# Dense tiles with all products of first weight parts ahead of second ones, inputs normalized one per tile, second weight parts on VectorE in the output, final stores on two queues

## The chip, the cores and the metric

The kernel runs on one core of a Trainium2 chip. Its engines are TensorE (PE in the profile; its weight loads are listed apart as PEld), VectorE (DVE), ScalarE (ACT), GpSimd (POOL) and SyncE (SP), which here only starts DMA transfers. Each engine works through its own list of instructions in a fixed order, and waits at an instruction until what it needs has been made by the others. The metric is the time of one execution on the device in microseconds; three runs of the kernel before took 1370.2, 1366.8 and 1364.27 us, the median is 1366.8 us.

## The reference

One step of a decoder with one layer, for 64 sample tokens (8 sequences of 8) and a prompt of 512 tokens, 576 in all; the width is 1024. Two mixers work on one projection and are added to the residual: a state-space mixer (Mamba-2, 16 heads of 64) and a delta-rule mixer (RWKV-7, 16 heads of 64). A gated feed-forward part (2816 wide) and a per-layer embedding follow.

```python
hn = rmsnorm(h, norm_mix)
z, xbc, dt, rw = split(hn @ w_in)
y_ssd  = rmsnorm_per_group(ssd(conv(xbc), dt) * silu(z)) * ssd_norm
u      = rw + (previous_row(rw) - rw) * shift_mu      # token shift
r, k, v, w_lo, a_lo, g_lo = split(u)
gate   = sigmoid(g_lo) @ g2
y_rwkv = (head_norm(wkv(r, k, v, decay(w_lo), a(a_lo))) + bonus) * gate
h = h + [y_ssd ; y_rwkv] @ w_out
h = h + (silu(rmsnorm(h) @ w_gate) * (rmsnorm(h) @ w_up)) @ w_down
h = h + sigmoid(rmsnorm(h) @ w_ple_gate) * (p @ w_ple_proj)
y = rmsnorm(h, norm_final)                            # and the new states
```

## The kernel before

Channels lie on the 128 partitions and the 576 tokens along the free axis; a matmul takes one half of the tokens (288 columns). A dense product keeps nearly full float32 precision by a split: a weight `w` and an input `x` are each written as a first part (rounded for TensorE) and a second part (what the rounding left out), and three products are added up in PSUM: first times first, first times second, second times first. `mm3` (L211 to L215) issues these three for one k-tile of 128 input channels and one half, so L213 and L214 use the first weight part `whi` and L215 the second, `wlo`.

`linear` (L217 to L224) makes one output tile of 128 channels. It fetches the weights in chunks of four k-tiles (`wload`, which calls `wsplit`, L189 to L199): SyncE starts a DMA into `raw` (three buffers), ScalarE copies it to `whi` (L92), and GpSimd and VectorE in turn subtract to make `wlo` (L198). `whi` and `wlo` have two buffers each, so the parts of the next chunk can be made while the products of this one run. PSUM holds two dense tiles at a time.

The stages are, with their places in the profiled span:

- Start (0 to 60 us). The input arrives, its first parts without the norm (`xu`) feed the first tiles, and the norm's factor is put in behind them (L341). `norm_x(n)` (L330) normalizes `n` input tiles on VectorE (L332) and splits them for the later dense tiles. `gate_in` makes the gate's input, `gates` (L416 to L426) eight small dense tiles from it.
- Mixers (60 to 690 us). Four quarters of heads. `fill` (L451) takes the next dense tile off a list and is called in between the mixers' steps; `fill_for` makes sure that the six tiles of a quarter are there. `outp` (L787) reads out the state of the delta rule. `head_norm` (L865 to L897) normalizes; that of the last quarter splits its result into the list `YR` (L897, second parts on GpSimd).
- Residual tiles of the delta-rule mixer (670 to 790 us), whose inputs partly come back from memory (`yl<-yr_d`).
- State-space mixer's end and its output (790 to 870 us). `scaled` (L1292) makes one output tile from four k-tiles, that is one chunk, scales it by `STD` (the tiles `bc`, L1297) and adds it to the residual `h` (L1298); `after` (L1275) splits the new `h` and squares it for the next norm. The loops at L1301 to L1305 run the first half of the inputs for all eight channels and then the second half.
- Feed-forward (870 to 1150 us, L1319 to L1333) and down projection (1150 to 1295 us, L1335 to L1341), whose 22 k-tiles make chunks of 4, 4, 4, 4, 4 and 2.
- Embedding gate (L1352 to L1392) in two parts, columns 0 to 320 and 320 to 576, and the final norm. All 16 stores of `yT` (L1392) start on SyncE's queue.

What the source lists is not what the engines execute in that order. A scheduler with a simulated timeline lays down the order of each engine's instructions when the kernel is built, and the buffers decide what may overlap. So a change in one place can alter the order everywhere behind it. ScalarE needs another table of functions when it goes from one group of functions to another (`ACT_TABLE_LOAD`); the square root of the norms has its own.

Of the kernel before, what the change touches and what calls it, by code (L numbers as in the profile page):

```python
# [8 lines left out]
F32 = mybir.dt.float32  # L9
# [65 lines left out]
def hybrid_step(ctx, tc, A):  # L75
# [15 lines left out]
    def act(out, in_, func=AF.Copy, scale=1.0, bias=0.0):  # L91
        S.activation(out, in_, func, bias=bias, scale=scale)  # L92

# [80 lines left out]
    wat = [0]  # L174
    flip = [0]

    def split(src, pool, tags, shape, lo_eng=None, hi=None, lo=None, hi_eng=None, **kw):
# [11 lines left out]
    def wsplit(src, n, hi=None, lo=None):  # L189
# [6 lines left out]
        flip[0] += 1  # L196
        eng = G if flip[0] % 2 else V
        eng.tensor_tensor(lo[:, 0:n], raw[:, 0:n], hi[:, 0:n].bitcast(F32), ALU.subtract)  # L198
# [18 lines left out]
    def linear(xs, ps):  # L217
        nk = len(xs)
        for k in range(0, nk, 4):
            b = min(4, nk - k)  # L220
            hi, lo = wload(b)
            for i in range(b):
                xh, xl = xs[k + i]
                mm3(ps, hi[:, i * P:(i + 1) * P], lo[:, i * P:(i + 1) * P], xh, xl, k + i == 0, k + i == nk - 1)  # L224

# [201 lines left out]

    norm_x(3)
    ugh = gate_in()
    norm_x(5)  # L430

# [287 lines left out]
    def chain(s):  # L719
# [67 lines left out]
        def outp(g):  # L787
            sv = suv(g)
            ow = outs[g]
            for jj in jj2:  # L790
                for e in range(2):
                    T.matmul(ow[H[e], jj], sv[:, jj, 1, e], Gt[:, g, jj, 1, e], start=False, stop=True,  # L792
                             skip_group_check=True)
            act(AR[:, :, g], ow)

# [70 lines left out]
    def head_norm(s, ahead=()):  # L866
# [18 lines left out]
        for jj in jj2:  # L885
# [10 lines left out]
            else:  # L896
                YR.append(split(y, xp, ("xhi", "xlo"), [P, NT], lo_eng=G))  # L897

# [5 lines left out]
    for s in Q:  # L904
        if s.q == 0:
            fill(2)
            gates(ugh)
        fill_for(s)
# [390 lines left out]

    st = {"x": []}  # L1300
    for c in range(8):  # L1301
        scaled(c, 0)
    for c in range(8):
        scaled(c, 1)
        after(c, hs[c], "norm_ffn", me, "xs", 8, st)  # L1305
    if not RS1:
        rs = rstd_of(st)
# [44 lines left out]
    for a, b in ((0, 320), (320, NT)):  # L1352
        n = b - a
        acc = None
        for c in range(8):
# [15 lines left out]
            V.tensor_tensor(t, ps, rs[:, a:b], ALU.mult)  # L1371
            act(t, t, AF.Sigmoid)
            V.tensor_tensor(t, t, PL[c][:, a:b], ALU.mult)  # L1373
# [11 lines left out]
        for c in range(8):  # L1385
# [4 lines left out]
            else:  # L1390
                V.scalar_tensor_tensor(h, h, par("norm_final", c), ps, ALU.mult, ALU.mult)
            nc.sync.dma_start(A["yT"][c, :, a:b], h)  # L1392

# [131 lines left out]
```

## Time and profile before

| what | value |
|---|---|
| median of three runs | 1366.8 us |
| the profiled execution | 1370.43 us, span 1368.7 us |
| TensorE busy, mean granted clock | 1259.1 us (92%), 0.947 |
| VectorE, ScalarE, GpSimd busy | 719.6, 577.4, 550.2 us |
| dense products (L213 to L215, all inputs) | the three costliest groups: 450.8, 447.9 and 447.7 us |
| `wlo` subtract (L198) | GpSimd 136 x 1344 ns, VectorE 136 x 724 ns |

The profiled execution is one of the slower ones of this kernel. Busy time of matmuls overlaps: a matmul is listed with 0.29 us though the next one starts sooner, so the spacing of the starts tells the rate. The clock is the one granted to TensorE, as a share of its higher level.

### The profile page before, as it was taken

What the parts mean: (1) busy time and instruction counts of PE and PEld (TensorE: products, weight loads), DVE (VectorE), ACT (ScalarE), POOL (GpSimd) and SP (SyncE); (2) the same over time, 40 slices, a digit from 0 to 9 for tenths busy, and PEclk for the clock granted to TensorE, in tenths of its full rate; (3) what the DMA queues carried; (4) which work ended last, traced back from release to release, by engine and by line L of the source; (5) the groups of instructions that cost most, each with busy time, mean ns of one, the idle gap of its engine ahead of it and who ended that gap; (6) DMA issues with size and microseconds to landing.
All of it is one profiled execution on the core that took longest, in us unless ns stands there. A gap on an engine that the chain in (4) does not pass through costs nothing.

```text
span 1368.7 us, 26325 instructions
## 1 busy us (share of the span) xinstructions
PE 1259.1 (92%) x10565; PEld 1160.4 (85%) x10565; DVE 719.6 (53%) x1333; ACT 577.4 (42%) x1148; POOL 550.2 (40%) x543
## 2 busy tenths in 40 slices
PE   6897999999989979899989979999999999999986
PEld 5786897789868857777779769999999999999985
DVE  7648766787687785843367676522222221111255
ACT  6565345634653553344425364432332332222253
POOL 5326414632454153133456676432332332334332
PEclk9997899899979989989999989999999999999998
DMA  4322342234223312362644532233232222222432
GB/s 162 124 70 62 85 119 60 81 100 128 61 90 91 101 58 84 88 209 82 189 145 142 183 97 71 70 85 79 84 85 81 83 85 77 82 80 79 148 92 69
DMA packets 94458, 135.56 MB, mean 99 GB/s; under 512 B 34704, under 2 KB 39056, under 8 KB 94336
## 3 DMA queue, kind: packets, MB, share of 16 engines
q1 hardware_dynamic: 94336, 133.88, 32.8%
q8 instruction: 83, 1.36, 0.4%
q14 instruction: 39, 0.32, 0.1%
HBM read 106.10 MB, written 27.75 MB: 98 GB/s over the span
## 4 chain that ended last, share of the span: by engine, by line
PE 60%; DVE 15%; ACT 5%; DMA 5%; issue 4%; POOL 3%; DVEq 0%; SPq 0%; ACTq 0%; POOLq 0%
PE lin L215 16%; PE lin L213 16%; PE lin L214 16%; DVE h L375 2%; DVE Tt L656 1%; DVE tmp L654 1%; DMA raw<-wts 1%; POOL wlo L198 1%; DVE suv L809 1%; PE cx L777 1%; PE lin L593 1%; PE cx L769 1%; DVE wlo L198 1%; PE cx L792 1%; DVE pg L1373 1%
## 5 line engine op out<-in xcount | busy, mean ns | idle before, releaser
L213 PE MATMUL lin<-xhi,whi 128*128 128x288 f32 (+1 forms) x1488 | 450.8, 303 | 3.3 <-ACT whi L92 2.2
L215 PE MATMUL lin<-xhi,wlo 128*128 128x288 f32 (+1 forms) x1488 | 447.9, 301 | 3.2 <-POOL wlo L198 2.2
L214 PE MATMUL lin<-xlo,whi 128*128 128x288 f32 (+1 forms) x1488 | 447.7, 301 | 1.0 <-POOL xlo L186 1.0
L198 POOL TENSOR_TENSOR wlo<-raw,whi 128x512 fp32r<-128x512 f32 x136 | 182.8, 1344 | 501.9 <-ACT whi L92 462.1
L92 ACT ACTIVATE whi<-raw 128x512 fp32r<-128x512 f32 (+1 forms) x272 | 168.8, 621 | 397.7 <-PE lin L214 341.1
L213 PEld LDWEIGHTS lin<-xhi,whi 128*128 128x128 f32 (+1 forms) x1488 | 281.4, 189 | 10.5 <-ACT whi L92 2.6
L215 PEld LDWEIGHTS lin<-xhi,wlo 128*128 128x128 f32 (+1 forms) x1488 | 282.3, 190 | 7.0 <-POOL wlo L198 2.8
L214 PEld LDWEIGHTS lin<-xlo,whi 128*128 128x128 f32 (+1 forms) x1488 | 281.9, 189 | 6.1 <-POOL xlo L186 2.1
L198 DVE TENSOR_TENSOR wlo<-raw,whi 128x512 fp32r<-128x512 f32 (+1 forms) x136 | 98.4, 724 | 167.4 <-ACT whi L92 164.8
L215 PE MATMUL lin<-ah,wlo 128*128 128x288 f32 x352 | 105.0, 298 | 0.9
L213 PE MATMUL lin<-ah,whi 128*128 128x288 f32 x352 | 104.0, 296 | 0.0
L214 PE MATMUL lin<-al,whi 128*128 128x288 f32 x352 | 103.8, 295 | 0.0
L215 PEld LDWEIGHTS lin<-ah,wlo 128*128 128x128 f32 x352 | 66.2, 188 | 3.2 <-POOL wlo L198 2.6
L214 PEld LDWEIGHTS lin<-al,whi 128*128 128x128 f32 x352 | 66.1, 188 | 0.0
L213 PEld LDWEIGHTS lin<-ah,whi 128*128 128x128 f32 x352 | 66.0, 187 | 0.0
L1332 DVE TENSOR_TENSOR sg<-lin,sg 128x576 f32<-128x576 f32 x22 | 16.7, 758 | 82.9 <-PE lin L215 81.7
L1327 DVE TENSOR_TENSOR sg<-lin,rstd 128x576 f32<-128x576 f32 x22 | 16.7, 758 | 69.3 <-PE lin L215 69.0
L654 DVE TENSOR_TENSOR tmp<-L,Tt 72x30 f32<-72x30 f32 (+14 forms) x120 | 48.9, 407 | 3.2
L656 DVE TENSOR_TENSOR Tt<-Tt,tmp 72x30 f32<-72x30 f32 (+14 forms) x120 | 46.1, 384 | 3.4
L213 PE MATMUL lin<-xu,whi 128*128 128x288 f32 x128 | 39.9, 313 | 8.5 <-ACT xu L92 6.9
L215 PE MATMUL lin<-xu,wlo 128*128 128x288 f32 x128 | 40.0, 314 | 7.3 <-DVE wlo L198 5.5
L186 POOL TENSOR_TENSOR al<-sg,ah 128x576 fp32r<-128x576 f32 x22 | 31.5, 1433 | 32.1 <-ACT ah L92 32.1
(370 smaller groups left out, 2513.6 us busy)
## 6 DMA issues: line engine op xcount, KB each, us to landing
raw<-wts SPq DMA_DIRECT2D x271, 256.0 KB, 2.6
S<-s_wkv SPq DMA_DIRECT2D x8, 512.0 KB, 5.1
hd<-s_ssm SPq DMA_DIRECT2D x8, 512.0 KB, 4.0
o_ssm_s<-hd SPq DMA_DIRECT2D x8, 512.0 KB, 2.9
xbc_d<-E SPq DMA_DIRECT2D x12, 288.0 KB, 2.1
x<-xT SPq DMA_DIRECT2D x8, 288.0 KB
gate_d<-g SPq DMA_DIRECT2D x8, 288.0 KB, 2.6
bv_d<-rw SPq DMA_DIRECT2D x8, 288.0 KB
```

The costliest lines, as they stand in the source:

```text
L92: S.activation(out, in_, func, bias=bias, scale=scale)
L186: eng.tensor_tensor(lo[:], src, hi[:].bitcast(F32), ALU.subtract)
L198: eng.tensor_tensor(lo[:, 0:n], raw[:, 0:n], hi[:, 0:n].bitcast(F32), ALU.subtract)
L213: T.matmul(ps[:, a:b], whi, xhi[:, a:b], start=first, stop=False)
L214: T.matmul(ps[:, a:b], whi, xlo[:, a:b], start=False, stop=False)
L215: T.matmul(ps[:, a:b], wlo, xhi[:, a:b], start=False, stop=last)
L375: V.scalar_tensor_tensor(h[:], E[:, i:i + 600], w(i), h[:], ALU.mult, ALU.add)
L593: T.matmul(ps[:, c:c + 128].rearrange("p (a t) -> p a t", a=2), s.BK[jj][H[e], g].rearrange("p a t -> p (a t)"), s.G[H[e], g, jj, :, e], s ...
L654: V.tensor_tensor(o, L[:, jx:jx + 1, jx + 1:32].to_broadcast([NB, jx, n]), Tt[:, 0:jx, jx:jx + 1].to_broadcast([NB, jx, n]), ALU.mult)
L656: V.tensor_tensor(Tt[:, 0:jx, jx + 1:32], Tt[:, 0:jx, jx + 1:32], o, ALU.subtract)
L1327: V.tensor_tensor(s_[:], ps, rs[:], ALU.mult)
L1332: V.tensor_tensor(s_[:], up, s_[:], ALU.mult)
```

## The change

Six edits:

- `linear` issues, for each chunk, the 16 products with the first weight part (both inputs, both halves, four k-tiles) and then the 8 with the second weight part. Before, each k-tile and half had its three products together. `mm3` stays in use for the gates and other small tiles.
- `norm_x(3)`, `gate_in`, `norm_x(5)` become `norm_x(1)`, `gate_in`, `norm_x(1)`, and the other six inputs are normalized one after each of the first quarter's six dense tiles. The gates come after the third of these tiles instead of after the second.
- While the output loops run, all `wlo` are made on VectorE (`only[0] = V`) instead of in turn with GpSimd.
- The last quarter's `YR` second parts are made on VectorE instead of GpSimd.
- A square root of one column (`root_ready`) is placed after the last `outp` of the last quarter, and after the last sigmoid of the second half, so that the table for the square root is loaded there.
- In the second half, stores of odd channels start on ScalarE's queue.

```diff
--- before.py
+++ after.py
@@ -89,7 +89,13 @@
         return f"{s}_{uid[0]}"
 
     def act(out, in_, func=AF.Copy, scale=1.0, bias=0.0):
-        S.activation(out, in_, func, bias=bias, scale=scale)
+        return S.activation(out, in_, func, bias=bias, scale=scale)
+
+    def root_ready(ins):
+
+        with tc.issue_after(ins.ins):
+            t = cp.tile([P, 1], F32, tag="rr", name=nm("rr"), bufs=2)
+            act(t[:], eps_t[:, 2:3], AF.Sqrt)
 
     lins, turn = [lin], [0]
 
@@ -173,6 +179,7 @@
 
     wat = [0]
     flip = [0]
+    only = [None]
 
     def split(src, pool, tags, shape, lo_eng=None, hi=None, lo=None, hi_eng=None, **kw):
         hi = hi if hi is not None else pool.tile(shape, F32R, tag=tags[0], name=nm(tags[0]), **kw)
@@ -194,7 +201,7 @@
             lo = wp.tile([P, 512], F32R, tag="wlo", name=nm("wlo"))
         act(hi[:, 0:n], raw[:, 0:n])
         flip[0] += 1
-        eng = G if flip[0] % 2 else V
+        eng = only[0] or (G if flip[0] % 2 else V)
         eng.tensor_tensor(lo[:, 0:n], raw[:, 0:n], hi[:, 0:n].bitcast(F32), ALU.subtract)
         return hi, lo
 
@@ -219,9 +226,14 @@
         for k in range(0, nk, 4):
             b = min(4, nk - k)
             hi, lo = wload(b)
+            w = [slice(i * P, i * P + P) for i in range(b)]
             for i in range(b):
-                xh, xl = xs[k + i]
-                mm3(ps, hi[:, i * P:(i + 1) * P], lo[:, i * P:(i + 1) * P], xh, xl, k + i == 0, k + i == nk - 1)
+                for c, d in HV:
+                    T.matmul(ps[:, c:d], hi[:, w[i]], xs[k + i][0][:, c:d], start=k + i == 0, stop=False)
+                    T.matmul(ps[:, c:d], hi[:, w[i]], xs[k + i][1][:, c:d], start=False, stop=False)
+            for i in range(b):
+                for c, d in HV:
+                    T.matmul(ps[:, c:d], lo[:, w[i]], xs[k + i][0][:, c:d], start=False, stop=k + i == nk - 1)
 
     def fsum(ps, w, x):
         for a, b in HV:
@@ -425,9 +437,9 @@
                 act(g[:], ps)
                 nc.sync.dma_start(gate_d[h * 4 + jj][:], g[:])
 
-    norm_x(3)
+    norm_x(1)
     ugh = gate_in()
-    norm_x(5)
+    norm_x(1)
 
 
     H = (slice(0, 64), slice(64, 128))
@@ -791,7 +803,9 @@
                 for e in range(2):
                     T.matmul(ow[H[e], jj], sv[:, jj, 1, e], Gt[:, g, jj, 1, e], start=False, stop=True,
                              skip_group_check=True)
-            act(AR[:, :, g], ow)
+            out = act(AR[:, :, g], ow)
+            if q == 3 and g == 8:
+                root_ready(out)
 
         def prompt_state(g):
             sv = suv(g)
@@ -894,7 +908,7 @@
             if q < 3:
                 nc.sync.dma_start(yr_d[j][:], yo)
             else:
-                YR.append(split(y, xp, ("xhi", "xlo"), [P, NT], lo_eng=G))
+                YR.append(split(y, xp, ("xhi", "xlo"), [P, NT], lo_eng=V))
 
     def inverse(s):
         solve(s)
@@ -902,9 +916,11 @@
         combine(s)
 
     for s in Q:
-        if s.q == 0:
-            fill(2)
-            gates(ugh)
+        for i in range(6) if s.q == 0 else ():
+            fill(1)
+            norm_x(1)
+            if i == 2:
+                gates(ugh)
         fill_for(s)
         prep(s)
         start_states(s)
@@ -1298,11 +1314,13 @@
         (V if g and c % 2 else G).tensor_tensor(hs[c][:], hs[c][:], t[:], ALU.add)
 
     st = {"x": []}
+    only[0] = V
     for c in range(8):
         scaled(c, 0)
     for c in range(8):
         scaled(c, 1)
         after(c, hs[c], "norm_ffn", me, "xs", 8, st)
+    only[0] = None
     if not RS1:
         rs = rstd_of(st)
     mix2.close()
@@ -1369,7 +1387,9 @@
             sq = ft("sq")[:, 0:n]
             h = hs[c][:, a:b]
             V.tensor_tensor(t, ps, rs[:, a:b], ALU.mult)
-            act(t, t, AF.Sigmoid)
+            sig = act(t, t, AF.Sigmoid)
+            if a and c == 7:
+                root_ready(sig)
             V.tensor_tensor(t, t, PL[c][:, a:b], ALU.mult)
             V.tensor_tensor(h, h, t, ALU.add)
             if c < 7:
@@ -1389,7 +1409,7 @@
                 G.tensor_tensor(h, h, rl, ALU.mult)
             else:
                 V.scalar_tensor_tensor(h, h, par("norm_final", c), ps, ALU.mult, ALU.mult)
-            nc.sync.dma_start(A["yT"][c, :, a:b], h)
+            (nc.scalar if a and c % 2 else nc.sync).dma_start(A["yT"][c, :, a:b], h)
 
 
 def pack(inp):
```

The order of the instructions moves in all stages. Three places follow; names are those of tiles, with a number that tells the instances apart, and `x4` at the end of a row means four instructions in a row that read alike.

TensorE's list at the end of the output, where the tiles of the last two channels are made (`lin_9677` and `lin_9718`; `yh` and `yl` are the first and second parts of the inputs), before:

```order
L214 MATMUL lin_9636<-yl_8639,whi_9639 128x288
L215 MATMUL lin_9636<-yh_8638,wlo_9640 128x288
L213 MATMUL lin_9677<-yh_8620,whi_9680 128x288
L214 MATMUL lin_9677<-yl_8621,whi_9680 128x288
L213 MATMUL lin_9718<-yh_8620,whi_9721 128x288
L214 MATMUL lin_9718<-yl_8621,whi_9721 128x288
L215 MATMUL lin_9677<-yh_8620,wlo_9681 128x288
L213 MATMUL lin_9677<-yh_8620,whi_9680 128x288
L214 MATMUL lin_9677<-yl_8621,whi_9680 128x288
L215 MATMUL lin_9677<-yh_8620,wlo_9681 128x288
```

The same place in the changed kernel (`lin_9679` and `lin_9720`):

```order
L232 MATMUL lin_9679<-yh_8640,whi_9682 128x288
L233 MATMUL lin_9679<-yl_8641,whi_9682 128x288
L232 MATMUL lin_9679<-yh_8640,whi_9682 128x288
L233 MATMUL lin_9679<-yl_8641,whi_9682 128x288
L236 MATMUL lin_9679<-yh_8622,wlo_9683 128x288 x4
L236 MATMUL lin_9679<-yh_8640,wlo_9683 128x288 x4
L232 MATMUL lin_9720<-yh_8622,whi_9723 128x288
L233 MATMUL lin_9720<-yl_8623,whi_9723 128x288
L232 MATMUL lin_9720<-yh_8622,whi_9723 128x288
L233 MATMUL lin_9720<-yl_8623,whi_9723 128x288
```

Before, the first two products of the last tile stand between the second and the third product of the tile ahead of it. Now a tile's first-part products end, its eight second-part products follow, and then the last tile begins.

VectorE's list at the start, from the first shift instruction on (`rw` is the shifted tile, `u` the dense tile with the norm's factor), before:

```order
L348 SCALAR_TENSOR_TENSOR rw_337<-sst,pv,rw_337 128x9
L349 SCALAR_TENSOR_TENSOR rw_337<-u_335,pv,rw_337 128x511
L351 SCALAR_TENSOR_TENSOR rw_337<-u_335,pv,rw_337 128x8x7
L186 TENSOR_TENSOR xlo_351<-x_200,xhi_350 128x576
L186 TENSOR_TENSOR xlo_361<-x_204,xhi_360 128x576
L348 SCALAR_TENSOR_TENSOR rw_427<-sst,pv,rw_427 128x9
L349 SCALAR_TENSOR_TENSOR rw_427<-u_425,pv,rw_427 128x511
L351 SCALAR_TENSOR_TENSOR rw_427<-u_425,pv,rw_427 128x8x7
L186 TENSOR_TENSOR xlo_442<-x_206,xhi_441 128x576
L186 TENSOR_TENSOR xlo_452<-x_216,xhi_451 128x576
L198 TENSOR_TENSOR wlo_573<-raw_570,whi_572 128x512
```

And in the changed kernel:

```order
L360 SCALAR_TENSOR_TENSOR rw_337<-sst,pv,rw_337 128x9
L361 SCALAR_TENSOR_TENSOR rw_337<-u_335,pv,rw_337 128x511
L363 SCALAR_TENSOR_TENSOR rw_337<-u_335,pv,rw_337 128x8x7
L193 TENSOR_TENSOR xlo_351<-x_200,xhi_350 128x576
L360 SCALAR_TENSOR_TENSOR rw_417<-sst,pv,rw_417 128x9
L361 SCALAR_TENSOR_TENSOR rw_417<-u_415,pv,rw_417 128x511
L363 SCALAR_TENSOR_TENSOR rw_417<-u_415,pv,rw_417 128x8x7
L193 TENSOR_TENSOR xlo_432<-x_202,xhi_431 128x576
L205 TENSOR_TENSOR wlo_518<-raw_515,whi_517 128x512
L193 TENSOR_TENSOR xlo_586<-x_206,xhi_585 128x576
L193 TENSOR_TENSOR xlo_828<-x_216,xhi_827 128x576
```

Four `xlo` stood ahead of `wlo_573`, which belongs to the second chunk of the fourth dense tile (`lin_539`). Now two stand ahead of `wlo_518`, of the first chunk of the fourth tile (`lin_514`).

ScalarE's list where the output begins (`rn` is the root of the norm, `bc_8502` the first scale row, `sg` and `er` belong to the state-space mixer), before:

```order
L92 ACT_TABLE_LOAD
L92 ACTIVATE rn_1331_8525<-d_8504,eps_t 128x5
L92 ACTIVATE bc_8502<-d_8503 128x448
L92 ACTIVATE bc_8613<-xs_6627 128x576
L92 ACTIVATE bc_8502<-d_8504 128x128
L92 ACTIVATE bc_8614<-xs_6629 128x576
L92 ACTIVATE sg_8589<-r_8587,tk_7180 128x128 x2
L92 ACT_TABLE_LOAD
L92 ACTIVATE er_8582<-r_8587 64x384
```

And in the changed kernel, where the scale row is `bc_8504`:

```order
L92 ACT_TABLE_LOAD
L92 ACTIVATE rn_1332_8527<-d_8506,eps_t 128x5
L92 ACTIVATE whi_9267<-raw_9265 128x512
L92 ACTIVATE sg_8591<-r_8589,tk_7182 128x128 x2
L92 ACT_TABLE_LOAD
L92 ACTIVATE er_8584<-r_8589 64x384
L92 ACTIVATE sg_8591<-sg_8591 128x256
L92 ACTIVATE bc_8504<-d_8505 128x448
L92 ACTIVATE bc_8615<-xs_6627 128x576
L92 ACTIVATE bc_8504<-d_8506 128x128
L92 ACTIVATE bc_8616<-xs_6629 128x576
```

The first scale row was copied right behind `rn`. Now a weight copy, two `sg`, a table load, `er` and another `sg` stand between them.

## Rows read from the trace of the kernel before

**Rows 1.** The page: busy time, share of span and count of each engine; chain of waits

```profile
PE 1259.1 (92%) x10565; PEld 1160.4 (85%) x10565; DVE 719.6 (53%) x1333; ACT 577.4 (42%) x1148; POOL 550.2 (40%) x543
...
PE 60%; DVE 15%; ACT 5%; DMA 5%; issue 4%; POOL 3%; DVEq 0%; SPq 0%; ACTq 0%; POOLq 0%
```

**Rows 2.** Three stretches: length, busy time (instructions) of PE, PEld, DVE, ACT, POOL, clock, DMA

```profile
40.00:60.00 20.00, 13.83 (x74) 12.52 (x75) 12.71 (x21) 12.40 (x23) 8.15 (x5) 0.83 0.36 118
180.00:680.00 500.00, 458.15 (x4415) 392.37 (x4414) 338.23 (x728) 237.15 (x540) 186.08 (x215) 0.92 0.34 102
790.00:870.00 80.00, 70.35 (x554) 66.39 (x552) 56.16 (x66) 41.43 (x75) 55.57 (x36) 0.94 0.27 73
```

**Rows 3.** Table of waits of TensorE, 80 to 780 us: total, times, longest

```profile
PE lin L215 <- POOL wlo L198: 2.2, 3, 1.1
```

**Rows 4.** Table of waits of TensorE's weight loads, down projection (1150 to 1296 us)

```profile
PEld lin L215 <- POOL wlo L198: 2.6, 7, 0.4
```

**Rows 5.** Timeline of VectorE, down projection: start, duration, engine, line, operation, operands, idle

```profile
1168.13 0.76 DVE L1339 TENSOR_TENSOR dn<-lin,rstd 128x576 f32<-128x576 f32 x1 [4.06 <-PE lin L215]
...
1186.12 0.76 DVE L1339 TENSOR_TENSOR dn<-lin,rstd 128x576 f32<-128x576 f32 x1 [4.06 <-PE lin L215]
...
1276.74 0.76 DVE L1339 TENSOR_TENSOR dn<-lin,rstd 128x576 f32<-128x576 f32 x1 [4.06 <-PE lin L215]
```

**Rows 6.** Timeline of all engines, end of the third down tile, start of the fourth

```profile
1203.24 0.30 PE L213 MATMUL lin<-ah,whi 128*128 128x288 f32 x1
...
1203.27 1.28 POOL L198 TENSOR_TENSOR wlo<-raw,whi 128x512 fp32r<-128x512 f32 x1 [5.11 <-ACT whi L92]
...
1204.18 0.29 PE L214 MATMUL lin<-al,whi 128*128 128x288 f32 x1
...
1204.61 0.40 PE L215 MATMUL lin<-ah,wlo 128*128 128x288 f32 x1
```

**Rows 7.** Timeline of all engines, start of the program

```profile
40.25 0.29 PE L214 MATMUL lin<-xu,whi 128*128 128x288 f32 x1
...
41.60 1.41 DVE L186 TENSOR_TENSOR xlo<-x,xhi 128x576 fp32r<-128x576 f32 x2
...
45.27 0.68 DVE L198 TENSOR_TENSOR wlo<-raw,whi 128x512 fp32r<-128x512 f32 x1
...
45.99 0.61 PE L215 MATMUL lin<-xu,wlo 128*128 128x288 f32 x1 [5.45 <-DVE wlo L198]
```

**Rows 8.** Timeline of all engines, last two channels of the output

```profile
857.59 0.61 ACT L92 ACTIVATE whi<-raw 128x512 fp32r<-128x512 f32 x1
...
858.26 0.40 PE L213 MATMUL lin<-yh,whi 128*128 128x288 f32 x1 [1.81 <-ACT whi L92]
...
859.47 0.40 PE L215 MATMUL lin<-yh,wlo 128*128 128x288 f32 x1 [0.68 <-POOL wlo L198]
...
860.67 0.44 PE L214 MATMUL lin<-yl,whi 128*128 128x288 f32 x1
...
864.15 0.29 PE L213 MATMUL lin<-yh,whi 128*128 128x288 f32 x1
```

**Rows 9.** Timeline of all engines, residual tiles and head norm of the last quarter

```profile
684.60 1.41 POOL L186 TENSOR_TENSOR xlo<-yl,xhi 128x576 fp32r<-128x576 f32 x1 [0.40 <-ACT xhi L92]
...
684.85 1.28 ACT L92 ACT_TABLE_LOAD   x1
```

**Rows 10.** Groups of VectorE by line, output stage; and one subtract

```profile
L1297 DVE TENSOR_TENSOR yl<-lin,bc 128x576 f32<-128x576 f32 x16 | 11.9, 754 | 16.2 <-PE lin L215 15.3 <-ACT bc L92 0.9
...
L1279 DVE SCALAR_TENSOR_TENSOR xlo<-h,pv,xhi 128x576 fp32r<-128x576 f32 x7 | 8.8, 1262 | 0.3 <-ACT xhi L92 0.2
...
820.55 1.93 DVE L198 TENSOR_TENSOR wlo<-raw,whi 128x512 fp32r<-128x512 f32 x1
```

**Rows 11.** Timeline of all engines, final stores

```profile
1361.98 2.44 DVE L1391 SCALAR_TENSOR_TENSOR h<-h,pv,lin 128x256 f32<-128x256 f32 x6 [1.20 <-ACT rs L92]
...
1362.49 3.77 SPq L1392 DMA_DIRECT2D yT<-h  x8
```

## Prediction

> **What bounds the kernel now.** I read the page first. TensorE is busy 92% of the span and carries 60% of the chain of waits, VectorE 15% [rows 1]. So only time in which TensorE stands still, or runs at its lower clock, is to be had. The table by stage says where that is: from 40 to 60 us TensorE is busy 13.83 of 20 us at a granted clock of 0.83, in the mixing stage (180 to 680 us) 458.15 of 500 at 0.92, in the output stage (790 to 870 us) 70.35 of 80 at 0.94 [rows 2]. The tables of waits then tell who ends the idle time. In the mixing stage second weight parts from GpSimd end only 2.2 us of it [rows 3]; the rest hangs on operands of the mixers, which this change leaves alone. Last, the timeline gives the spacing: the eight matmuls of dense tiles from 1203.24 to 1204.18 start 0.94 / 7 us apart, which the rounded starts put at 0.133 to 0.136 [rows 6]; I use 0.133. Whether the weight part changes between two of them makes no difference there. Placing products of one weight part side by side buys no rate; it can only move the moment at which a part is needed.
>
> **Down projection.** All seven waits of this stage end on `wlo` made by GpSimd, 2.6 us together [rows 4]. VectorE takes a finished tile at 1168.13 and the next at 1186.12, 17.99 us later, and 1276.74 after five more, 18.12 each [rows 5]; the 132 products alone are 132 x 0.133 = 17.56 us. The chunks are 4, 4, 4, 4, 4 and 2 k-tiles long, so behind the short one only 12 products (1.6 us) hide the making of the next pair, of which GpSimd's subtract alone takes 1.28 us. It starts at 1203.27, and the product that wants it at 1204.61, 0.43 us after its predecessor instead of 0.13 [rows 6]. With 16 first-part products ahead (2.1 us instead of 0.27) `wlo` is in time by 1.5 us. Removed: at least the waits, 2.6 us, at most the periods, 0.43 + 6 x 0.56 = 3.8 us. I take -3.5, near the periods, since they hold what a stop costs behind it too. Nothing is late behind it: the first part was there on time each time.
>
> **What the new order costs.** A chunk's second inputs (`xl`) are now wanted every 0.53 us per k-tile instead of every 0.80. Where inputs, not weights, are late, the last input has eight second-part products more behind it, less two that were there: 6 x 0.133 = 0.8 us. Such a place is the residual tiles near 684 us, whose inputs GpSimd makes one after the other at 1.41 us [rows 9]. Bounds 0 and +2 (two or three such tiles); I take +0.8, one tile.
>
> **Start.** TensorE stops after 40.25 and goes on at 45.99, for a second part that VectorE makes at 45.27, behind the normalized inputs, `xlo` and shift instructions [rows 7]. The change has two `xlo` of 0.70 us fewer ahead of the next such `wlo`, so it would end at 45.95 - 1.4 = 44.55. But by the new order TensorE stops on it after 160 dense products, where before it stopped after 170: ten products are 1.3 us, and the gain is nothing. The gate products, which followed the second tile, now follow the third, and their input gets a tile of cover. The stretch's clock of 0.83 costs 0.17 x 20 = 3.4 us [rows 2]; if the stop became half as long, some of that and 1 to 2 us of the stop would come back: -5. If the later halves of `X` come too late for the tiles that follow, as late as one normalize, split and subtract each: +3. I take -1.
>
> **Mixing stage.** Of [rows 3] the 2.2 us should go. But all static orders behind the start are dealt out anew, and 500 - 458.15 = 41.85 us of idle time hang on them. A fifth either way is 8 us, both ends; I take -2, since the mixers' own instructions are the same.
>
> **Head norm and residual inputs.** The Sqrt table load at 684.85 (1.28 us) stands ahead of the scale that the last group waits for [rows 9]; it moves ahead of that group's sums. GpSimd's 1.41 us for the last quarter's `xlo` become VectorE's 0.70 [rows 7, 9]. Together up to -2.0; 0 is the other end, if products cover both. I take -1.5.
>
> **Output stage.** The tiles of the last two channels were interleaved. At 858.26 TensorE had stood idle for 1.81 us, because ScalarE made `whi` only at 857.59 behind work that waits for GpSimd; at 859.47 for 0.68 us, for GpSimd's `wlo`. From 860.67 to 864.15 fourteen matmuls ran 0.249 us apart, the lower of the two clocks (1.2 of 2.4 GHz) [rows 8]. That is 1.81 + 0.68 + 14 x (0.249 - 0.133) = 4.1 us. The new order has whole tiles one after the other and every second part on VectorE: -4.1 if nothing else is late. Against that, ScalarE's copies of the first scale row (`bc`) now stand behind a weight copy (0.61), two preparations and a table load (1.28): up to 2.9 us later with the order's two short ones, and VectorE's first scaling and TensorE's decay products wait for them. Half can hide, since two tiles are in flight: +1.5. VectorE takes over eight subtractions: 8 x 0.68 = 5.4 us if GpSimd is quiet, 8 x 1.93 = 15.4 us if each meets it as the one at 820.55 did [rows 7, 10]. VectorE is busy 56.16 of 80 us there [rows 2], which leaves room for either, so I put it beside its own idle time, at 0. Term: -2.6; bounds -5 and +18 (third rival).
> The Trainium skill says in "SBUF — State Buffer", section "SBUF: two separate sides", that VectorE with two SBUF inputs and GpSimd share one port pair as an exclusive lock, and the second one fully blocks. The rows agree: 1.93 us is 0.68 and 1.28 one behind the other. By that rule a subtract moved to VectorE takes less of the shared time, 8 x (1.28 - 0.68) = 4.8 us in all, and the term would lie nearer to -5.
>
> **Tail.** SyncE issues eight stores in 3.77 us, 0.47 each, while VectorE makes its six tiles in 2.44 us and is done at 1364.42; the last issue ends at 1366.26 [rows 11]. On two queues the last can start behind its tile, some 1.4 us sooner, and that is the most. ScalarE's issue time is in no row; if a third of the stores' time came on top, at half the number each, the last would come 0.5 us later, the other end. I take -1.2.
> The Trainium skill ("DMA: Bandwidth & Descriptors", section "Issuing engines are not separate DMA queues") says that all issuing engines feed the same 16 DMA engines, and a second one saves issue time alone. The gap of 3.77 to 2.44 us is such time, so by that rule nothing comes beyond the 1.4.
>
> **Sum.** -3.5 + 0.8 - 1 - 2 - 1.5 - 2.6 - 1.2 = -11.0 us. The profiled execution took 1370.43 us around its span of 1368.7 and would come to 1359.4. The median of the three runs is 1366.8, 3.6 us lower, so I forecast 1356.
>
> **Rivals.**
> - *The stops move on.* A wait on `wlo` at the start turns into one on the same engine a tile later, and the mixers take back the rest. For it: by the new order the stop at 40 us does not go away. Against it: the down projection has no mixers beside it. Then the down projection and half the tail stand: -3.5 - 0.6 = -4.1, 1363.
> - *More than the sum, through the clock.* The clock of 0.92 costs 500 x 0.08 = 40 us in the mixing stage [rows 2]. If fewer stops lift it by a quarter, 10 us come on top: 1346. For it: the slow matmuls at 860 us come right behind two stops [rows 8]. Against it: the mixers' own small products stay.
> - *VectorE sets the pace of the output.* Place: 809 to 862 us. Price: 8 x 1.93 + 2.9 = 18.3 us in the place of -2.6, 20.9 more than in the sum: 1377, slower than before. It decides as soon as VectorE's work per tile (scaling 0.75, next input 1.26 [rows 10], `wlo`) exceeds a tile's 24 x 0.133 = 3.2 us. For it: with 1.93 for `wlo` that work is 3.9 us. Against it: with 0.68 it is 2.7, and GpSimd, which makes the 1.93, has eight instructions less.
>
> **How the numbers follow.** The forecast gets 0.50 (its own range 1348 to 1363), the stops that move on 0.27, the clock 0.12, VectorE's pace 0.11. About 0.5% (6.8 us) is what a measurement of this kernel can tell from no change: below 1360.0 is faster, above 1373.6 slower. Faster: 0.85 x 0.50 + 0.2 x 0.27 + 0.12 = 0.60; slower: 0.9 x 0.11 = 0.10; the rest, 0.30, is the same. The range goes from 1341, the clock case with half the mixing stage's -8 in it, to 1371, past the moved stops; about 0.1 stays above it, and as much below.
>
> **What would show it.** Down projection: tiles 17.5 us apart and no wait on `wlo`; if they stay at 18.1, its step is wrong. Start: a stop of 4 to 6 us that ends on VectorE's `wlo` between 43 and 45 us. Output: no matmul at the lower clock from 858 us on, and the first scale row's copies behind a table load; a stop of over 3 us on VectorE's `yl` or `wlo` between 812 and 850 us would speak for the third rival. Tail: four issues of the last eight on each queue, and the last of them 1 us after its tile instead of 1.84. A mixing stage longer or shorter by over 8 us would make the forecast wrong.

## The result, and the profile after

The changed kernel takes 1373.53 us in the median of eight runs (1369.6 to 1376.89), the kernel before 1367.74 (1364.27 to 1370.2): a ratio of 1.0041, interval 1.0025 to 1.0057. It is slower by a little, where 1356 was forecast. The profiled execution took 1374.64 us, its span is 1372.9, 4.2 us longer than that of before.

The page first, then three stretches by the clock of the span, then the third of the four quarters of heads by itself, from the first product of its triangular solve to the last product of its state steps (columns as in [rows 2]).

```profile
PE 1268.2 (92%) x10565; PEld 1171.7 (85%) x10565; DVE 729.8 (53%) x1343; ACT 580.6 (42%) x1150; POOL 542.2 (39%) x533
...
PE 65%; DVE 15%; DMA 4%; ACT 4%; issue 3%; POOL 1%; SPq 0%; DVEq 0%; ACTq 0%; POOLq 0%
```

```profile
40.00:60.00 20.00, 14.56 (x92) 14.09 (x92) 15.20 (x26) 9.53 (x19) 8.75 (x6) 0.83 0.22 67
180.00:680.00 500.00, 463.35 (x4363) 399.20 (x4361) 330.95 (x717) 234.93 (x531) 181.02 (x211) 0.89 0.33 98
790.00:870.00 80.00, 68.53 (x545) 63.39 (x542) 64.36 (x86) 42.04 (x80) 47.05 (x29) 0.94 0.29 85
472.10:572.90 100.80, 87.16 (x826) 69.51 (x828) 69.01 (x154) 43.09 (x98) 33.35 (x41) 0.77 0.28 83
```

The third quarter in the kernel before:

```profile
481.00:567.40 86.40, 71.54 (x762) 57.95 (x764) 65.64 (x145) 36.95 (x89) 35.12 (x39) 0.86 0.26 79
```

TensorE is busier than before over the same 10565 matmuls: 9.1 us more. Nothing was added to its work, so it ran more of it at the lower clock: in the mixing stage the granted clock is 0.89 instead of 0.92 [rows 2]. Most of that lies in the third quarter, which takes 100.8 us instead of 86.4 at a clock of 0.77 instead of 0.86: of the 30.8 us more that the clock is at the lower level in the mixing stage, 21.5 are there (the ledger below).

The late places answer to their rows as follows. Down projection (VectorE's timeline; compare [rows 5]):

```profile
1178.18 0.76 DVE L1357 TENSOR_TENSOR dn<-lin,rstd 128x576 f32<-128x576 f32 x1 [4.32 <-PE lin L236]
1195.78 0.76 DVE L1357 TENSOR_TENSOR dn<-lin,rstd 128x576 f32<-128x576 f32 x1 [4.32 <-PE lin L236]
1213.38 0.76 DVE L1357 TENSOR_TENSOR dn<-lin,rstd 128x576 f32<-128x576 f32 x1 [4.32 <-PE lin L236]
...
1283.78 0.76 DVE L1357 TENSOR_TENSOR dn<-lin,rstd 128x576 f32<-128x576 f32 x1 [4.32 <-PE lin L236]
1303.05 0.75 DVE L1357 TENSOR_TENSOR dn<-lin,rstd 128x576 f32<-128x576 f32 x1
```

The tiles are 17.60 us apart, the last one 19.27, and the table of TensorE's waits is empty for this stage, where it had seven [rows 4]. Start (timeline; compare [rows 7]):

```profile
44.49 0.68 DVE L205 TENSOR_TENSOR wlo<-raw,whi 128x512 fp32r<-128x512 f32 x1
...
45.23 1.09 PE L236 MATMUL lin<-xu,wlo 128*128 128x288 f32 x3 [6.21 <-DVE wlo L205]
```

The stop is still there, 6.21 us on VectorE's `wlo`. Output (TensorE's waits, then ScalarE's timeline ahead of the first one):

```profile
822.61 1.67 PE L1188 MATMUL d<-bc,hin 128*128 128x128 f32 x12 [3.19 <-ACT bc L92]
```

```profile
819.78 1.28 ACT L92 ACT_TABLE_LOAD   x1
821.08 0.49 ACT L92 ACTIVATE er<-r 64x384 f32<-64x384 f32 x1
821.57 0.42 ACT L92 ACTIVATE sg<-sg 128x256 f32<-128x256 f32 x1
822.01 0.54 ACT L92 ACTIVATE bc<-d 128x448 f32<-128x448 f32 x1
```

TensorE waits 3.19 us for the scale row behind the table load. In the kernel before the same products waited 0.16 us for it:

```profile
809.23 2.83 PE L1172 MATMUL d<-bc,hin 128*128 128x128 f32 x12 [0.16 <-ACT bc L92]
```

The two stops of [rows 8] at the output's end are gone, and nothing there runs at the lower clock. Final stores (timeline; compare [rows 11]):

```profile
1366.85 2.44 DVE L1411 SCALAR_TENSOR_TENSOR h<-h,pv,lin 128x256 f32<-128x256 f32 x6 [1.20 <-ACT rs L92]
...
1367.36 2.00 SPq L1412 DMA_DIRECT2D yT<-h  x4
1367.75 1.95 ACTq L1412 DMA_DIRECT2D yT<-h  x4
```

Four issues on each queue, the last done at 1369.70, 0.41 us after VectorE's last tile instead of 1.84; from the start of that last group of VectorE to the end of the span it is 6.05 us instead of 6.7.

A ledger of the profiled executions, cut at the same instructions (length in us; in brackets how much of it TensorE's clock was at the lower level; no bracket: none of it):

| stretch | before | after |
|---|---|---|
| start to the first quarter's solve | 190.4 (30.7) | 189.4 (34.1) |
| to the third quarter's solve | 290.6 (44.4) | 282.6 (47.8) |
| third quarter | 86.4 (24.2) | 100.8 (45.7) |
| to the last state product | 106.7 (13.3) | 109.6 (19.2) |
| to the output's first scaling | 135.8 (14.2) | 140.8 (23.9) |
| output, to the feed-forward's first tile | 78.0 (6.2) | 74.3 (0) |
| feed-forward | 280.2 | 280.5 |
| down projection | 127.2 | 124.9 |
| embedding gate, to VectorE's first tile that is stored | 45.1 (3.4) | 42.2 (3.4) |
| last stores to the end | 28.3 (9.8) | 27.6 (9.4) |

The sum is the 4.2 us of the spans but for rounding: from the output on 9.3 us are won, and 13.3 lost ahead of it.

### The profile page after: what moved, and what is told of

Its sections match the earlier page's. It is cut to its first block, busy times and chain, and to the rows that moved or that the text cites. A ratio compares the mean times of both kernels' runs of the same rounds, so it can differ in the third digit from the quotient of the medians.

```text
span 1372.9 us, 26325 instructions
## 1 busy us (share of the span) xinstructions
PE 1268.2 (92%) x10565; PEld 1171.7 (85%) x10565; DVE 729.8 (53%) x1343; ACT 580.6 (42%) x1150; POOL 542.2 (39%) x533
## 4 chain that ended last, share of the span: by engine, by line
PE 65%; DVE 15%; DMA 4%; ACT 4%; issue 3%; POOL 1%; SPq 0%; DVEq 0%; ACTq 0%; POOLq 0%
PE lin L232 16%; PE lin L233 16%; PE lin L236 15%; PE lin L605 2%; DVE tmp L666 2%; DVE Tt L668 1%; DVE suv L823 1%; PE cx L841 1%; DVE h L387 1%; DVE wlo L205 1%; DMA raw<-wts 1%; PE cx L781 1%; DMA L<-Ld 1%; PE lin L220 1%; PE cx L789 1%
## 5 line engine op out<-in xcount | busy, mean ns | idle before, releaser
L232 PE MATMUL lin<-xhi,whi 128*128 128x288 f32 x1440 | 408.8, 308 | 7.0 <-ACT lo L92 4.0
L233 PE MATMUL lin<-xlo,whi 128*128 128x288 f32 x1440 | 406.7, 304 | 1.8 <-DVE xlo L1295 1.1
L232 PEld LDWEIGHTS lin<-xhi,whi 128*128 128x128 f32 x1440 | 279.6, 194 | 13.1 <-ACT lo L92 5.2
L233 PEld LDWEIGHTS lin<-xlo,whi 128*128 128x128 f32 x1440 | 278.6, 193 | 6.8 <-POOL xlo L193 1.9
L236 PE MATMUL lin<-xhi,wlo 128*128 128x288 f32 x1440 | 235.8, 301 | 0.0
L236 PEld LDWEIGHTS lin<-xhi,wlo 128*128 128x128 f32 x1440 | 206.0, 191 | 3.0 <-issue 1.5
L205 DVE TENSOR_TENSOR wlo<-raw,whi 128x512 fp32r<-128x512 f32 x144 | 102.3, 711 | 131.5 <-PE lin L236 97.3
L236 PE MATMUL lin<-ah,wlo 128*128 128x288 f32 x352 | 54.8, 296 | 0.0
L605 PE MATMUL lin<-G,bk 64*128 64x128 f32 x288 | 41.8, 404 | 9.8 <-POOL bk L577 8.9
L605 PEld LDWEIGHTS lin<-G,bk 64*128 64x128 f32 x288 | 34.0, 286 | 16.9 <-POOL bk L577 11.7
```

Source lines behind the costliest of these rows:

```text
L232: T.matmul(ps[:, c:d], hi[:, w[i]], xs[k + i][0][:, c:d], start=k + i == 0, stop=False)
L233: T.matmul(ps[:, c:d], hi[:, w[i]], xs[k + i][1][:, c:d], start=False, stop=False)
L236: T.matmul(ps[:, c:d], lo[:, w[i]], xs[k + i][0][:, c:d], start=False, stop=k + i == nk - 1)
L605: T.matmul(ps[:, c:c + 128].rearrange("p (a t) -> p a t", a=2), s.BK[jj][H[e], g].rearrange("p a t -> p (a t)"), s.G[H[e], g, jj, :, e], s ...
```

## The experiments

Three theories stood after the result. A: the spread inputs and gates rearrange the mixers. B: the new order of products itself costs in the mixing stage. C: the loss lies in the late edits. The first four kernels tell them apart; each has part of the change.

**Only the new order of products** (`linear` as in the change).

> Only the dense tiles' new order (16 first-part products, then 8 second-part ones per chunk); inputs, gates, output and stores as before. Theory B (the new order itself lets the mixing stage, 280 to 600 us, fall to the lower clock for longer: 185 us of lower clock in the changed kernel against 148): the mixing stage loses about 10 us here too, the down projection and the FFN gain 3, so 1372 to 1376 us, 4 to 8 slower than before, over 175 us at the lower clock. Theory A (the spread inputs and gates at the start rearrange the mixers): no loss here, the down projection's 3 us and some of the output's remain, 1361 to 1365. Theory C (the loss is in VectorE's second parts in the output and the table loads): 1362 to 1365 as well.

1376.71 us, ratio 1.0047 (1.0029 to 1.0066). The third quarter took 95.1 us with 42.0 at the lower clock, the down projection 125.8. As B has it, 0.7 us above its range.

**Everything but the new order.**

> Everything of the change but the new order of products. Theory B: no loss in the mixing stage, down projection as before (18.1 us a tile), tail 1 us better: 1363 to 1368. Theory A: the whole mixing loss of about 10 us without the down projection's gain: 1374 to 1380. Theory C: 2 to 6 us slower than before from 690 us on, 1370 to 1374.

1375.4 us, 1.0046 (1.0029 to 1.0062). The third quarter took 98.1 us (53.6 at the lower clock) though `linear` was the old one. As A has it, and B alone is not enough.

**Only the inputs and the gates.**

```diff
-    norm_x(3)
+    norm_x(1)
     ugh = gate_in()
-    norm_x(5)
+    norm_x(1)
...
-        if s.q == 0:
-            fill(2)
-            gates(ugh)
+        for i in range(6) if s.q == 0 else ():
+            fill(1)
+            norm_x(1)
+            if i == 2:
+                gates(ugh)
```

> Only the inputs normalized one per tile and the gates behind the third tile. Theory A: the mixing loss is here, 1374 to 1380. Theories B and C: within 4 us of before, 1364 to 1371.

1384.37 us, 1.0114 (1.0092 to 1.0135): near three times the loss of the whole change, and more than A expected. Third quarter 95.0 us, 36.2 at the lower clock.

**Only the late edits** (second parts on VectorE in the output, the last quarter's second inputs, the preloads, the stores).

> Only the late edits: second parts on VectorE in the output, the last quarter's second inputs on VectorE, the two square-root preloads, stores on two queues. Theory C: slower from 690 us on by 4 to 6 us less 1 us of the tail, 1370 to 1374. Theories A and B: up to 690 us as before, the first scale row 2 to 3 us late, the tail 1 us better: 1366 to 1369.

1360.05 us, 0.9934 (0.9913 to 0.9956). C is out: the late edits are a gain, and a larger one than any theory had. Up to the third quarter's end the order of all engines is that of the kernel before; the quarter begins and ends within 0.2 us of where it did there, and took 86.3 us. The profiled execution, 1365.99 us, is the slowest of the six: its span is 4.4 us shorter than that of the kernel before, half of the 9 us (0.66%) by which the runs are faster. Where the other half lies is not shown.

Two unlike edits, e1 and e3, cost the same stage. That made a fourth theory, D: whatever deals the mixers' order out anew costs there, through the clock.

**The late edits, and the new order of products from the output on** (in short):

```diff
+    grouped = [False]
...
+            if grouped[0]:
+                # products as in the change
+                continue
...
+    grouped[0] = True
     st = {"x": []}
```

> The late edits of the fourth experiment, and the new order of products from the output stage on only; start and mixers keep the order of the kernel before. Theory D (the mixing stage loses through the granted clock as soon as its order is dealt out anew, whatever edit does it; the new order itself is good where weights were the wait): mixing stage as before (lower clock about 24 us between 500 and 600 us), down projection 17.5 us a tile, so 3 to 4 us below the fourth experiment's 1360, 1355 to 1358. Theory B (the new order costs wherever it stands): no better than 1360, the output and FFN lose what the down projection gains.

1359.05 us, 0.9935 (0.9912 to 0.9957): 1 us above what was expected, and faster than both kernels. Third quarter 81.9 us; down projection 124.7; output 72.9. The feed-forward, 3.5 us longer in e4 (283.7), is back at 280.5. 3.0 of the 3.5 us lie right at its start: VectorE's first two scalings there (`sg<-lin,rstd`) start 5.70 us apart in e4, 2.67 in e5 and in the kernel before. The engines that make the second parts of its weights come in the same turn in all three. The medians of e4 and e5 are 1 us apart, less than can be told.

**Kernel before, the turn of the two engines flipped.**

```diff
-    flip = [0]
+    flip = [1]
```

> Kernel before, with one edit that costs nothing by itself: the turn between GpSimd and VectorE for second parts begins with VectorE instead of GpSimd, so that each weight part changes places. Theory D: the mixing stage's order is dealt out anew, and it loses 5 to 15 us by the lower clock, 1372 to 1384, with 35 us or more of it between 500 and 600 us. Theory B (new order of products): nothing to lose here, 1364 to 1372.

1384.84 us, 1.0123 (1.0096 to 1.015), for an edit that adds no work and has nothing to do with the change. Third quarter 97.9 us. In its size as D has it, 0.8 us above the range; the lower clock, 28.8 us there, was less than D asked, and 44 dense products more had been moved into the quarter. From the first quarter's solve to the last state product this kernel takes 16.0 us more. Of these TensorE stands still for 5.3 (45.5 us instead of 40.2); it is busy at the lower level for 84.5 us instead of 71.8, and half of the 12.7 more, 6.3 us, is lost by estimate. So the clock is less than half of this loss.

**Only the spread inputs, the gates where they were** (against the third experiment):

```diff
-            if i == 2:
+            if i == 1:
                 gates(ugh)
```

> Kernel before, with the inputs normalized one per tile, the gates behind the second tile as before. The third quarter's order of dense products is that of the third experiment. Theory D: the same loss as there, 1379 to 1386. If the gates' place was the reason: 1364 to 1371.

1378.75 us, 1.0072 (1.0046 to 1.0099); third quarter 97.6 (53.1 at the lower clock). Just under the range that was expected, but the same loss.

**Only the gates, behind the third tile.**

```diff
-            fill(2)
+            fill(3)
             gates(ugh)
```

> Kernel before, with the gates behind the third tile and the inputs normalized as before. The third quarter's order is that of the kernel before. Theory D: no loss, 1364 to 1371, with 24 us of lower clock between 500 and 600 us. If the gates' place was the reason for the third experiment's loss: 1379 to 1386.

1366.45 us, 0.9997 (0.9974 to 1.002). Third quarter 86.7 us. The gates are not the reason.

**The whole change with the turn flipped.** By the order alone the dense products of the third quarter stood where the kernel before has them.

> The whole change, with the turn between GpSimd and VectorE for second parts begun on VectorE. By the order alone the third quarter has its dense products where the kernel before has them (none ahead of the fifth state step, then 14, 21, 44, 22, 42; the whole change puts 12 and 12 ahead of the first two steps). Theory D (which deal of the order the third quarter gets decides over its clock): the third quarter takes 82 to 88 us instead of 100.8 and the kernel 1356 to 1364, faster than before. Theory B (the new order of products in the mixing stage costs by itself): the third quarter stays at 95 us and more, 1370 to 1376.

1369.42 us, 1.0003 (0.9989 to 1.0018), and the third quarter 95.5 us (44.3 at the lower clock). A miss: the place of the dense products alone does not decide, and the quarter took what theory B had for it. That D could name the winner from the order is refuted. That the flip moves the time, here by 4 us downward, is not.

**The fifth experiment with the gates later.**

> The fifth experiment with the gates behind the third tile as well. The third quarter's order is that of the kernel before. Theory D: third quarter 82 to 88 us, 1355 to 1359, up to 2 us below the fifth experiment; slower than 1363 would speak against it.

1360.15 us, 0.9925 (0.9901 to 0.9949), 1 us above the expected range and no better than e5. The third quarter took 85.7 us, as expected.

**Second parts on VectorE in the output alone** (`only[0] = V` around the two loops).

> Kernel before, with the second parts on VectorE while the output loops run, and nothing else. The output's part of the prediction by itself: output stage 2.6 us shorter than before by my sum (bounds 5 shorter and 18 longer), up to 5 by the ledger of the fourth experiment (77.9 to 71.8 us with the feed-forward's first tile); the feed-forward 3 us longer, as there, since the turn of the second parts is another one: 1363 to 1367.

1364.74 us, 0.9971 (0.9954 to 0.9987). Output 71.6 us instead of 78.0, feed-forward 283.7 instead of 280.2: 6.4 won, 3.5 given back. It is not the turn, as expected, that takes them back: it is the same as before, and 3.0 of the 3.5 us again lie between the first two scalings.

**Head norm alone** (second inputs of the last quarter on VectorE, the first preload).

> Kernel before, with the last quarter's second inputs on VectorE and the square-root preload after the last state step. Predicted 1.5 us shorter between the third quarter's end and the output; by the fourth experiment's ledger 1.4. Everything else as before: 1365 to 1368.

1364.5 us, 0.9969 (0.995 to 0.9988). The stretch to the output's first scaling is 136.0 us, as before (135.8), so the profile does not show the 1.5 us where I put them; the runs are faster by 0.1% to 0.5%, with a median 0.5 us under the expected range.

The next two add a stop, and no new order of products.

**A stop in the third quarter of the kernel before**, one of GpSimd's outer products made twice:

```diff
-                    G.tensor_tensor(um[:], sv[:, jj, 1, e]...
+                    for _ in range(2 if q == 2 and jj == e == 0 else 1): G.tensor_tensor(um[:], sv[:, jj, 1, e]...
```

> Kernel before, with one of GpSimd's four outer products of the third quarter's first state step (each 1.5 us) made twice. Theory D (the third quarter sits close to the lower clock; a stop of 1 to 2 us more in its first steps is enough): the quarter takes 95 us or more instead of 86.4, with over 35 us of lower clock from 480 to 600 us, and the kernel 1375 to 1382, 7 us and more for 1.5 us of work. If the order of the dense products was what counted, and not stops: 1.5 us longer at most, 1368 to 1371.

1384.31 us, 1.0092 (1.0071 to 1.0113): some 13 us by the ratio, 15 by the medians, for 1.5 us on GpSimd, and 2.3 us above D's range. The stop shows in TensorE's timeline as a wait for the products of GpSimd, and behind it as a longer wait for the states' transfer:

```profile
501.13 1.98 PE L827 MATMUL cx<-um,bkt 128*64 128x512 f32 x4 [3.16 <-POOL um L824]
...
520.70 0.60 PE L714 MATMUL cb<-G,S 64*64 64x16 f32 x6 [4.03 <-DMA S<-s_wkv]
```

The same waits in the kernel before, where there were two short ones for GpSimd:

```profile
502.52 1.07 PE L827 MATMUL cx<-um,bkt 128*64 128x512 f32 x2 [0.44 <-POOL um L824]
504.04 1.07 PE L827 MATMUL cx<-um,bkt 128*64 128x512 f32 x2 [0.44 <-POOL um L824]
...
519.53 2.76 PE L714 MATMUL cb<-G,S 64*64 64x16 f32 x48 [2.28 <-DMA S<-s_wkv]
```

and in the table by stage, the quarter with its stop:

```profile
478.00:579.20 101.20, 78.73 (x761) 63.30 (x762) 72.17 (x159) 37.41 (x89) 35.04 (x40) 0.76 0.24 72
```

Of the 14.8 us more in this quarter TensorE stands still for 7.6 (22.5 us instead of 14.9); it is busy at the lower level for 38.7 us instead of 20.1, and half of the 18.6 more, 9.3 us, is lost by estimate. So waiting and clock have a like part in it, and D, which put all of it on the clock, is borne out for one part only.

**The same stop in the second quarter** (`q == 1`):

> The same doubled product in the second quarter, where TensorE has 344 dense products behind the state steps instead of 144; 11 rows of TensorE's list change places. Theory D: the third quarter keeps its order and its 82 to 88 us; the second loses 2 us at most: 1366 to 1371. If any new deal of the order costs: 1374 to 1382.

1373.5 us, 1.0024 (1.0006 to 1.0043), above the expected range; the profiled execution, 1370.4 us of span, has 2.1 us more in the second quarter and this third one:

```profile
481.60:566.60 85.00, 70.92 (x760) 57.63 (x762) 65.66 (x145) 36.96 (x89) 34.92 (x39) 0.85 0.26 80
```

So by the profiles the same instruction costs 15 us in the quarter with 144 dense products behind its state steps and 2 in the one with 344. In e13 the order within the quarter changed as well (some 120 of its 762 matmuls stand elsewhere in TensorE's list), so the stop and the order are not apart: the 15 us may be the order's.

**The changed kernel once more.**

> The changed kernel once more, for a second profile of the same order. Theory D: third quarter again over 95 us with 35 us or more of lower clock; its time falls by about half a microsecond for each microsecond of lower clock less. If the first profile was a chance: 82 to 88 us in this one.

1374.23 us, 1.0033 (1.0012 to 1.0053). The third quarter repeats:

```profile
468.90:571.60 102.70, 89.67 (x826) 72.22 (x826) 68.98 (x154) 43.29 (x98) 34.51 (x41) 0.74 0.26 81
```

## Why the prediction was wrong

**The step that failed is the mixing stage.** I took -2 for it "since the mixers' own instructions are the same", with 8 us either way, and set the price by idle time. From the first quarter's solve to the last state product it came to +9.3, which is the sign that I had named for a wrong forecast, and the idle time did not grow: TensorE stands still for 37.5 us of this stretch instead of 40.2. Laid over the records of the clock, it is busy at the lower level for 102.1 us instead of 71.8. If half of such time is lost, which is an estimate from the two levels, the 30.3 us more cost 15 us; by the group shown below, which takes 1.8 times as long, it is 13. Either is more than the whole loss.

In the third quarter TensorE stands still for 13.6 us instead of 14.9, and is busy for 87.16 us instead of 71.54. Of that 42.2 us fall into the lower level instead of 20.1; half of the 22.1 more, 11 us, is lost to it. The other 4.5 us are work, 168 dense products instead of 144 the most of it, that the stretch ahead was spared (282.6 us instead of 290.6). What this looks like is best seen on one group of the mixers' products, sixteen in a row, in the timeline of before and of after:

```profile
515.27 1.16 PE L593 MATMUL lin<-G,bk 64*128 64x128 f32 x16
```

```profile
526.96 2.08 PE L605 MATMUL lin<-G,bk 64*128 64x128 f32 x16
```

Such a group takes 1.8 times as long. In the kernel before the clock was full from 499 to 519 us, with stops of at most 0.5 us, and fell at the one of 2.28 us shown above; in the changed one it fell at 510.2 behind three stops of 2.8 us together and stayed low until 534:

```profile
507.34 0.33 PE L804 MATMUL cx<-G,suv 128*64 128x64 f32 x2 [1.06 <-ACT suv L92]
508.56 0.45 PE L815 MATMUL cx<-suv,bkt 128*64 128x64 f32 x8 [0.89 <-DVE suv L797]
510.07 1.33 PE L781 MATMUL cx<-suv,G 128*128 128x128 f32 x4 [0.82 <-DVE suv L823]
```

This is repeatable, not chance: the eight profiles with the mixers' order of before or nearly so (before, e4, e5, e8, e10, e11, e12, e14) have 81.9 to 86.7 us in that quarter and 17 to 25 at the lower clock; the nine with another order (after twice, e1 to e3, e6, e7, e9, e13) 95.0 to 102.7 and 29 to 54. Two of them, e6 and e13, come from edits that have nothing to do with the change. At one order the time of the quarter goes with the clock, too: with TensorE's order of before, but for four matmuls, e5 took 81.9 us with 16.6 at the lower clock and e8 86.7 with 24.6; e2, e3 and e7, whose order is the same, took 98.1, 95.0 and 97.6 with 53.6, 36.2 and 53.1. What was not tried, because nothing here sets it, is the clock set by hand at one fixed order; and which order keeps it high cannot be read from the lists, as e9 shows.

The traces hold seven orders of this quarter: that of the kernel before, and six others (the change, e1, e6, e9, e13, and the one of e2, e3 and e7). Only the first is fast. So it can be said as well that the kernel before had a lucky order as that every new one is a bad one; no run tells the two apart. How far the new order of products costs there by itself also stays open: every kernel with it in the mixers also has another order.

I had the row for it (0.92 in [rows 2]) and used it in one direction only, for a rival in which the clock rises. The rival that ended slower was put in the output, where the profile before showed room. Between the -11.0 of the sum and the +4.2 of the profiles lie 15.2 us: 11.3 are this stage, 5.7 the residual tiles and the head norm below, and the rest comes to some 2 us the other way.

**The start** (-1): -1.0, which is luck. The stop stayed, as the order said, with 6.21 us a little longer than the 4 to 6 named, and ended at 45.2, a little later than the 44.55 worked out. But this stretch takes 190.3 to 192.4 us in the profiles whose start is that of before (before, e4, e5, e11 to e14), 188.3 in e15, the changed kernel once more, and 193.7 and 193.5 in e3 and e7, which have its new inputs without its order of products; 1 us cannot be told from that.

**Residual tiles** (+0.8) **and head norm** (-1.5): +5.0 together, 9.7 us more of it at the lower clock. e4, with the head norm's edits, is 1.4 shorter, e12 no shorter, e1, with the new order, 4.4 longer. The lower clock varies here by 16 us among kernels with the mixers' order of before (e8 11.6, e5 27.3), so the terms cannot be told from it.

**The output** (-2.6): -3.7, with both halves as described: a wait of 3.19 us for the scale row instead of 0.16, and the two stops at the end gone. The third rival did not come: e11 alone wins 6.4. VectorE's subtractions took 0.80 us in the mean, near the short price.
By the Trainium skill's rule on the shared port ("SBUF — State Buffer", section "SBUF: two separate sides") the term would lie nearer to -5 than to -2.6. The changed kernel's -3.7 lies between the two and the 6.4 of e11 beyond them, and no run here shows the port by itself.

**The down projection** (-3.5): -2.3. The waits went; the first seven tiles are 0.39 to 0.52 us closer, 3.0 us in six spacings, and the last one, 19.27 us instead of 18.54, gave 0.7 back. Mis-sized by 1.2.

**The tail** (-1.2): -0.7. The last issue comes 1.4 us closer to its tile, as worked out, but the end only 0.7: the span ends 3.2 us behind the last issue instead of 2.4, and why is not shown.
The Trainium skill's sentence that a second issuing engine saves issue time alone ("DMA: Bandwidth & Descriptors", section "Issuing engines are not separate DMA queues") fits: no run shows more than that.

**Not in the sum:** the embedding gate, 45.1 to 42.2. Kernels with the old order of products have 42.9 to 45.2 us there, those with the new one 41.5 to 43.8; the cause was not looked for, and that it made up for part of the miss is luck.

## What to carry to other kernels

Where a scheduler lays down the order, an edit at the start is an edit everywhere: price the stage with the least slack against a reordering first, by its granted clock as well as by its idle time, and do not call it unchanged because its instructions are. Put such an edit behind the delicate stage if it can be put there; the late half of this change, by itself, takes 0.65% off (e5, 1359.05 us), and the whole of it adds 0.4%.

## What was not expected of the hardware

A busy TensorE is no sign that the time is well used: at the lower clock the mixers' small products fill the timeline (from 515 to 530 us of the changed kernel TensorE is busy all the time at a granted clock of 0.50). One instruction of 1.5 us more on GpSimd, with the new order that came of it, costs the kernel before 13 us (e13). And the spread between runs of one kernel goes with the clock too: the 29 runs of before beside e9 to e12 have a correlation of -0.78 between time and mean granted clock, and among them the shortest is 1363.1 us at 0.949, the longest 1373.37 at 0.940.
